# Four edits to a one-core decoder layer: part of product P2 next to P1 in the down projection, both parts of the compressed probabilities in one matmul, six row loads on ScalarE's queue, T sums written later

## The chip, the cores and the metric

The kernel runs on one core of a Trainium2 chip. The metric is device time in microseconds (us), the median of a few executions. The engines are named as in the profile: PE is TensorE's matmul, PEld its weight load, DVE is VectorE, ACT is ScalarE, POOL is GpSimd, SP is SyncE, whose queue issues most DMAs; "SPq" and "ACTq" are the queues of DMAs of SP and ACT.

## The reference

One decoder layer on x of 1024 rows by 1024 columns, all in float32: two attention mixers side by side, an output projection, a ConvFFN, and a gated per-layer embedding. Cut to what the change touches:

```
h = rmsnorm(x, g_pre_mix);  proj = h @ w_in
# NSA: 8 heads in 2 groups, three branches; the compressed one:
k_cmp, v_cmp = gelu(blocks(k) @ w1 + b1) @ w2, the same for v   # 63 blocks, head width 64
p_cmp = softmax(q k_cmp^T * scale - alibi) * mask;  o_cmp = p_cmp @ v_cmp
...                                              # selected and window branch, MLA, merge
x = x + rmsnorm(merged @ w_o, g_post_mix)
h = rmsnorm(x, g_pre_ffn)
u = causal_dwconv(h @ w_up, w_conv) + b_conv;  a, v = split(u)   # 2816 columns each
x = x + rmsnorm((gelu(a) * v) @ w_down, g_post_ffn)
e = p @ w_ple;  gate = sigmoid(x @ w_ple_gate)
x = x + rmsnorm(e * gate, g_ple)
```

## The kernel before

**Products in parts.** Every float32 operand of a large product is split into two rounded parts, hi and lo. ACT copies hi (`split_evac`, L308; for weights L106), DVE subtracts it for lo (L309; for weights L107), and `mm3` (L303 to L305) issues three matmuls: hi by hi, hi by lo, lo by hi. The three lines of `mm3` so stand for nearly all dense work of PE. DVE's row `wlo` or `wll` or `pl` is always the second half of such a split, and PE cannot use the part before it is there.

**Order.** The instructions of each engine come from a scheduler that orders the program by its own timeline; the source's order is an input to it, not the result. Tiles are taken from pools with a fixed number of buffers. PSUM tiles are `big` (two banks), `one`, `pT`, `oT`, `sc`.

**T sums.** The merge gates are computed by a seven-product (Strassen-like) scheme. Its sums T1 and T2 are made by `t_first(k)`, T3 and T4 by `t_second(k)`, for k from 0 to 3, on DVE and ACT, next to the projections of MLA's keys and values (`mla_k`, `mla_v`, some 120 to 190 us into the span). `st` is the tile into which MLA's projections are evacuated.

**Attention.** Units are one tile of 128 query rows by one group, with four heads (512 columns). `front` transposes the probabilities into PSUM (`pT`, L960) and splits them into `ph` and `pl`; `back` (L969, L970) multiplies both by the values and adds into `oT`. The unit's branch b = 0 is the compressed one: 64 rows of probabilities, and `Vc`, whose columns 0 to 63 hold the hi part of the values and columns 64 to 127 the lo part. There are 16 such units (8 row tiles by 2 groups).

**From w_o to the ConvFFN.** For eight tiles of 128 rows, in the order 4, 5, 6, 7, 0, 1, 2, 3: the row tile of x is loaded (`xt`, two buffers, L1402), `merged @ w_o` is accumulated, ACT squares it (L1359) for the norm, DVE multiplies by the norm and by `gpo` (L1410), adds `xt` (L1411), ACT squares `xt`, DVE multiplies by `gpf` (L1414), and PE transposes the result (L1370). `gpo` and `gpf` are rows of 1024 that are broadcast to 128 partitions by their loads (L1351, L1352, 512 KB each). Weights come through a ring of raw buffers, loaded on SP's queue (L81).

**Down projection.** A seven-product scheme on 2 by 2 blocks: P1, P5, P6, P3, P7, P4, P2, each of NJ = 11 units; a unit is a 128-deep slice, 12 matmuls of 128 by 512, into four banks. P1 is A11 B11 and P2 is A12 B21; their sum is the block c11 of the result. For each unit, `load` brings the blocks (through `wraw`, 3 buffers, or `QA`, `QS`, `GB`, which stay), `early_sums` makes the sums that P5, P6 and P7 need (L1544, on DVE; two for a P5 unit), and `ready` splits (ACT L308, DVE L309 `wlo`). After a product its four banks are added to or copied to `yacc`. Products P1, P6, P7, P2 take two `big` tiles, the others one `big` and two `one`. During P4 the weights of the gate (`wpg_items`) begin to come; after P4 the pool `qs` is closed, and the PLE inputs `praw`, `wlh`, `wll`, `pth`, `ptl` take its place; P2 runs beside their splits and transposes (`last_units`, `ple_in`, `fprep`). Then follow the PLE products and the gate's products.

Of the kernel before, what the change touches and what calls it, by code (L numbers as in the profile page):

```python
# [17 lines left out]
T = 1024  # L18
# [257 lines left out]
def tile_hybrid_layer(ctx: ExitStack, tc: tile.TileContext, x, p, positions, g_pre_mix, w_in,  # L276
# [679 lines left out]
    def front(u, key, cols, a, m=128):  # L956

        pT = bank().rearrange("p (a b) -> p a b", b=128)
        for r in range(a, 4):
            nc.tensor.transpose(pT[:m, r], cols(r), ident)  # L960
        tq = PL["tq"]
        ph = tq([128, 4, 128], F32R, "ph", bufs=3)
        pl = tq([128, 4, 128], F32R, "pl", bufs=3)
        split_evac(ph[:m, a:], pl[:m, a:], pT[:m, a:])
        u.hold[key] = (ph[:m, a:], pl[:m, a:])

    def back(u, key, oT, v, a, first, last):
        ph, pl = u.hold.pop(key)
        nc.tensor.matmul(oT[:, a:], v, ph, start=first, stop=False)  # L969
        nc.tensor.matmul(oT[:, a:], v, pl, start=False, stop=last)  # L970
# [6 lines left out]
    def nsa_unit(i, g, b):  # L977
# [107 lines left out]
        def t_back(j):  # L1085
            def run():
                if b == 1 and j == 0:
                    st["oT"] = new_oT()
                kb = k0 // 128 + j
                v = Vc[g][:64] if b == 0 else VV[kb // 4][:, kb % 4, 2 * (b - 1) + g]  # L1090
# [260 lines left out]
    nc.sync.dma_start(gpo, bcast_row(g_post_mix, D))  # L1351
    nc.sync.dma_start(gpf, bcast_row(g_pre_ffn, D))  # L1352
# [45 lines left out]
    for t in (4, 5, 6, 7, 0, 1, 2, 3):  # L1398
# [3 lines left out]
        nc.sync.dma_start(xt, x[0, ts, :])  # L1402
# [245 lines left out]

    def down_product(pi, per_unit):
        p_ = DOWN[pi]  # L1650
        if pi % 2:
# [4 lines left out]
        for j in range(NJ):  # L1656
            n = pi * NJ + j
# [4 lines left out]
            for m in range(2 * (n - 7), min(NJ, 2 * (n - 6))) if 7 <= n <= 12 else ():  # L1662
                early_sums(NJ + m)
            if n >= 13:
                early_sums(n + 9)
            ready(n + 4)
            per_unit(j)
            if n < 4 or n >= 15:
                load(n + 7)
            for m in range(2 * (n - 4), min(NJ, 2 * (n - 3))) if 4 <= n <= 9 else ():  # L1670
                load(NJ + m)
# [36 lines left out]
    for pi in range(1, 5):  # L1708
# [16 lines left out]
    down_product(5, lambda j: take(wpg_items[j // 2:j // 2 + 1]) if j % 2 and j < 10 else None)  # L1725
    qs.close()
# [16 lines left out]
    pp = Pool("pp", side="left")  # L1743
    praw = pp([128, NT, 256], F32, "praw")
    nc.sync.dma_start(praw, p[0, 0].rearrange("(t q) c -> q t c", q=128))
    wlh, wll = pp([128, 2, D], F32R, "wlh"), pp([128, 2, D], F32R, "wll")
    pth, ptl = pp([128, 2, T], F32R, "pth"), pp([128, 2, T], F32R, "ptl")
    for k, it in enumerate(ple_items):
        it.alloc = into(wlh[:, k], wll[:, k])
    ORDER = (4, 5, 6, 7, 0, 1, 2, 3)  # L1750
    for t in ORDER[:2]:
        x2_load(t)

    def ple_in(t):
        ps = one().rearrange("p (a b) -> p a b", b=128)
        for k in range(2):
            nc.tensor.transpose(ps[:, k], praw[:, t, k * 128:(k + 1) * 128], ident)
        ts = slice(t * 128, (t + 1) * 128)
        split_evac(pth[:, :, ts], ptl[:, :, ts], ps[:, :2])

    def last_units(j):
        if j in (1, 2):
            take(ple_items[j - 1:j])
        if j in (3, 5):
            fprep(ORDER[j // 2 - 1])
        if 6 <= j <= 9:
            ple_in(ORDER[2 * (j - 6)])
            ple_in(ORDER[2 * (j - 6) + 1])

    down_product(6, last_units)  # L1770
# [88 lines left out]
```

## Time and profile before

| | before |
|---|---|
| median of 3 runs | 1765.52 us (1764.72 to 1765.54) |
| profiled execution, its time | 1762.18 us |
| its span | 1760.5 us |
| its granted TensorE clock, mean | 0.994 |
| instructions | 23428 |
| busy PE, DVE, ACT, POOL | 1700.8, 1261.3, 853.0, 300.9 us |

Of the profiled execution's 1762.18 us, 1760.5 are the span of the trace; the 1.7 us around it are the same for any kernel here. The rows that the prediction reads from this trace stand below, numbered. In a timeline row "[1.40 <-DVE wlo L309]" means that the engine stood idle for 1.40 us before this instruction, and what ended the wait. PE's duration of one 128x512 matmul reads 0.39 us because matmuls are pipelined; in an unbroken run one starts every 0.23 us.

### The profile page before, as it was taken

To read this page: it belongs to the slowest core of one execution; us is meant where nothing else is said; L and a number is where in the kernel's file an instruction comes from. 1 tells how busy PE (TensorE), PEld (TensorE's weight loads), DVE (VectorE), ACT (ScalarE), POOL (GpSimd) and SP (SyncE) were. 2 spreads that over 40 slices of the span, in tenths; PEclk is the share of its full clock that TensorE was granted. 3 is DMA by queue.
4 is the path that set the end of the run, shared out by engine and by line. 5 is a ranking of instruction groups with operands and counts; after the bars stand their busy time and mean duration, and the time that the engine had idled before them with its cause. 6 is when DMAs were issued, how large, how long until landed. Compare 5 with 4: busy or idle time off the path is not lost.

```text
span 1760.5 us, 23428 instructions
## 1 busy us (share of the span) xinstructions
PE 1700.8 (97%) x8477; PEld 1390.7 (79%) x8477; DVE 1261.3 (72%) x1986; ACT 853.0 (48%) x1532; POOL 300.9 (17%) x435
## 2 busy tenths in 40 slices
PE   8999999999999999998999999999999998999998
PEld 6777888887777787886778877888888876887886
DVE  6577645238889777777754797888888789768553
ACT  6434433236777676666442454444444443335321
POOL 3000023014555553333211000000000000001111
PEclk9999999999999999999999999999999999999999
DMA  5176242100003236757362122232222292538111
GB/s 197 52 245 234 85 121 61 36 30 13 1 1 90 73 84 174 165 145 188 123 227 84 49 72 85 72 96 73 84 86 82 84 357 73 168 105 287 50 60 48
DMA packets 166670, 191.93 MB, mean 109 GB/s; under 512 B 13348, under 2 KB 116188, under 8 KB 166556
## 3 DMA queue, kind: packets, MB, share of 16 engines
q1 hardware_dynamic: 159452, 180.91, 33.1%
q10 hardware_dynamic: 7104, 9.54, 1.6%
q8 instruction: 67, 1.10, 0.3%
q14 instruction: 47, 0.39, 0.1%
HBM read 142.96 MB, written 47.45 MB: 108 GB/s over the span
## 4 chain that ended last, share of the span: by engine, by line
PE 80%; DVE 9%; DMA 6%; ACT 3%; issue 2%; POOL 1%; SPq 1%; DVEq 0%; POOLq 0%; ACTq 0%
PE big L304 9%; PE big L303 9%; PE big L305 9%; PE pT L303 6%; PE pT L305 6%; PE pT L304 6%; PE pT L960 5%; PE one L303 3%; PE one L304 3%; PE one L305 3%; PE oT L970 3%; PE oT L969 3%; DVE wlo L309 1%; PE sc L1023 1%; PE sc L1016 1%
## 5 line engine op out<-in xcount | busy, mean ns | idle before, releaser
L345 POOL TENSOR_SCALAR stat<-stat 128x1 f32<-128x1 f32 (+1 forms) x48 | 19.8, 412 | 892.1 <-ACT yn L1359 622.6
L308 ACT ACTIVATE ph<-pT 128x512 fp32r<-128x512 f32 (+1 forms) x244 | 130.2, 556 | 60.6 <-PE pT L960 52.5
L309 DVE TENSOR_TENSOR pl<-pT,ph 128x512 fp32r<-128x512 f32 (+1 forms) x244 | 149.6, 629 | 13.6 <-ACT ph L308 12.0
L303 PE MATMUL big<-hh,rh 128*128 128x512 f32 x380 | 148.2, 390 | 2.5 <-ACT e L220 1.0
L304 PE MATMUL big<-hl,rh 128*128 128x512 f32 x380 | 148.0, 389 | 0.0
L305 PE MATMUL big<-hh,rl 128*128 128x512 f32 x380 | 147.5, 389 | 0.0
L944 DVE TENSOR_REDUCE mx<-sc 128x1 f32<-128x640 f32 (+7 forms) x128 | 106.6, 835 | 32.1 <-PE sc L1023 22.3
L308 ACT ACTIVATE rh<-S 128x512 fp32r<-128x512 f32 x96 | 60.2, 629 | 110.3 <-PE big L304 78.0
L1482 DVE SCALAR_TENSOR_TENSOR u<-C,wcT,u 128x1024 f32<-128x1024 f32 x88 | 110.9, 1279 | 3.7 <-ACT u L1478 3.2
L304 PE MATMUL big<-wlo,whi 128*128 128x512 f32 x242 | 96.3, 398 | 9.3 <-DVE wlo L309 9.1
L303 PE MATMUL pT<-hh,whi 128*128 128x512 f32 x256 | 100.9, 394 | 3.0 <-DVE Vc L309 1.5
L308 ACT ACTIVATE rh<-wraw 128x512 fp32r<-128x512 f32 x80 | 50.0, 630 | 108.8 <-PE big L304 47.1
L305 PE MATMUL pT<-hh,wlo 128*128 128x512 f32 x256 | 100.7, 393 | 0.5 <-DVE wlo L107 0.5
L304 PE MATMUL pT<-hl,whi 128*128 128x512 f32 x256 | 100.3, 392 | 0.0
L305 PE MATMUL big<-whi,wlo 128*128 128x512 f32 x242 | 94.5, 390 | 0.0
L303 PE MATMUL big<-whi 128*128 128x512 f32 x242 | 90.8, 391 | 1.5 <-ACT whi L308 1.5
L303 PEld LDWEIGHTS big<-hh,rh 128*128 128x128 f32 x380 | 71.3, 188 | 18.6 <-ACT e L220 1.5
L304 PEld LDWEIGHTS big<-hl,rh 128*128 128x128 f32 x380 | 71.3, 188 | 15.1 <-DVE hl L309 0.4
L305 PEld LDWEIGHTS big<-hh,rl 128*128 128x128 f32 x380 | 71.3, 188 | 14.7
L309 DVE TENSOR_TENSOR rl<-S,rh 128x512 fp32r<-128x512 f32 x96 | 65.6, 686 | 19.5 <-ACT rh L308 19.5
L308 ACT ACTIVATE whi<-wraw 128x1024 fp32r<-128x1024 f32 x40 | 42.2, 1059 | 54.9 <-DVE wraw L1544 22.2
L304 PEld LDWEIGHTS big<-wlo,whi 128*128 128x128 f32 x242 | 45.4, 188 | 24.5 <-DVE wlo L309 15.5
(553 smaller groups left out, 4928.9 us busy)
## 6 DMA issues: line engine op xcount, KB each, us to landing
wraw<-in_w_up_dram SPq DMA_DIRECT2D x44, 512.0 KB, 3.9
wraw<-in_w_in_dram SPq DMA_DIRECT2D x24, 512.0 KB, 4.1
g<-gm_d SPq DMA_DIRECT2D x48, 256.0 KB, 4.1
wraw<-in_w_down_dram SPq DMA_DIRECT2D x47, 256.0 KB, 3.2
g_d<-u SPq DMA_DIRECT2D x22, 512.0 KB, 2.6
wraw<-g_d SPq DMA_DIRECT2D x36, 256.0 KB, 3.2
xt<-in_x_dram SPq DMA_DIRECT2D x16, 512.0 KB, 7.0
gm_d<-gms ACTq DMA_DIRECT2D x16, 512.0 KB, 2.6
```

What stands on the lines that cost most here:

```text
L303: nc.tensor.matmul(ps, lh, rh, start=start, stop=False, skip_group_check=more)
L304: nc.tensor.matmul(ps, lh, rl, start=False, stop=False, skip_group_check=more)
L305: nc.tensor.matmul(ps, ll, rh, start=False, stop=stop, skip_group_check=more)
L308: nc.scalar.activation(hi, ps, AF.Copy)
L309: nc.vector.tensor_sub(lo, ps, f32(hi))
L345: nc.gpsimd.tensor_scalar(st, st, EPS, None, op0=OP.add)
L944: nc.vector.tensor_reduce(u.nm[:, r:r + 1], src, axis=AX.XY, op=OP.max, negate=True)
L960: nc.tensor.transpose(pT[:m, r], cols(r), ident)
L969: nc.tensor.matmul(oT[:, a:], v, ph, start=first, stop=False)
L970: nc.tensor.matmul(oT[:, a:], v, pl, start=False, stop=last)
L1016: nc.tensor.matmul(ps[:, si, :w], qb[:, r], KB[b - 1][g][:, k0 + o:k0 + o + w], start=True, stop=False)
L1482: nc.vector.scalar_tensor_tensor(u[s], C[s][:, 2 - sh:2 - sh + T], wcT[:, 2 - sh, ch:ch + 1], u[s], op0=OP.mult, op1=OP.add)
```

## The change

Four edits, which do not touch each other:

- T sums: `t_first(0)` to `t_first(3)` are called later in the source.
- Compressed probabilities: DVE writes the lo part of the 64 rows into partitions 64 to 127 of `ph`, and `Vc` holds its columns twice, in rows 0 to 62 and 64 to 126; one matmul over 128 rows takes the place of two over 64.
- Row loads: `gpo`, `gpf` and the `xt` loads of tiles 4 and 5 are issued from ScalarE's queue.
- Down projection: P2's first 5 units stand right behind P1 and are added into P1's banks; its last 6 units stay at the end. P1 alone is copied to c21 first, P1 plus the 5 units to c11. The work that was spread beside 11 units of P2 is spread beside P4 and the last 6.

```diff
@@ T sums
     for i in range(4):
         for f in (mla_k(i, 0), mla_v(2 * i), mla_k(i, 1), mla_v(2 * i + 1)):
             f()
-        t_first(i)()
+        if i == 3:
+            t_first(0)()
         early.pop(0)()
+    t_first(1)()
...
     gates7 = Seven(nc, W, gate_pairs, ringA, BA, mm3, split_evac)
+    t_first(2)()
+    early.pop(0)()
+    t_first(3)()
+    early.pop(0)()
     for k in range(4):
         t_second(k)()
-        if k % 2:
-            early.pop(0)()
@@ compressed probabilities
-            split_evac(Vc[g][:63, 0:64], Vc[g][:63, 64:128], ps[:63, :64])
+            for o in (0, 64):
+                split_evac(Vc[g][o:o + 63, 0:64], Vc[g][o:o + 63, 64:128], ps[:63, :64])
...
+        if m == 64:
+
+            nc.scalar.activation(ph[:64], pT[:64], AF.Copy)
+            nc.vector.tensor_sub(ph[64:128], pT[:64], f32(ph[:64]))
+            u.hold[key] = [ph]
+            return
...
-        nc.tensor.matmul(oT[:, a:], v, ph, start=first, stop=False)
-        nc.tensor.matmul(oT[:, a:], v, pl, start=False, stop=last)
+        parts = u.hold.pop(key)
+        for j, part_ in enumerate(parts):
+            nc.tensor.matmul(oT[:, a:], v, part_, start=first and not j, stop=last and j == len(parts) - 1)
@@ row loads
-    nc.sync.dma_start(gpo, bcast_row(g_post_mix, D))
-    nc.sync.dma_start(gpf, bcast_row(g_pre_ffn, D))
+    nc.scalar.dma_start(gpo, bcast_row(g_post_mix, D))
+    nc.scalar.dma_start(gpf, bcast_row(g_pre_ffn, D))
...
-        nc.sync.dma_start(xt, x[0, ts, :])
+        (nc.scalar if 4 <= t < 6 else nc.sync).dma_start(xt, x[0, ts, :])
@@ down projection
-    DOWN = ("P1", "P5", "P6", "P3", "P7", "P4", "P2")
-    NJ = NF // 2
-    UNITS = [(p_, j) for p_ in DOWN for j in range(NJ)]
+    NJ, NP2 = NF // 2, 5
+    DOWN = [("P1", range(NJ)), ("P2", range(NP2))] + [(p_, range(NJ)) for p_ in ("P5", "P6", "P3", "P7", "P4")]
+    DOWN.append(("P2", range(NP2, NJ)))
+    UNITS = [(p_, j) for p_, js in DOWN for j in js]
...
+        p_, js = DOWN[pi]
+        more = pi == 1
+        if pi % 2 == 0 and pi:
             b = big()
             banks = [b[:, 0], b[:, 1], one(), one()]
-        else:
+        elif not more:
             banks = [b[:, h] for b in (big(), big()) for h in range(2)]
...
-                mm3(banks[t], hi[:, 0, lt], lo[:, 0, lt], hi[:, 1], lo[:, 1], j == 0, j == NJ - 1)
+                mm3(banks[t], hi[:, 0, lt], lo[:, 0, lt], hi[:, 1], lo[:, 1], i == 0 and not more,
+                    i == len(js) - 1, more)
...
             if p_ == "P1":
-                nc.scalar.activation(c11, ps, AF.Copy)
+                nc.scalar.activation(c21, ps, AF.Copy)
...
-                nc.vector.tensor_tensor(c21, c11, ps, op=OP.add)
+                nc.vector.tensor_tensor(c21, c21, ps, op=OP.add)
...
+            elif more:
+                nc.scalar.activation(c11, ps, AF.Copy)
...
-    down_product(6, last_units)
+    down_product(6, fourth)
+    down_product(7, last_units)
```

Three places show what the scheduler makes of it. On DVE, where MLA's projections are evacuated (`st`) and `t_first` makes T1 and T2 (L705 to L709), the changed kernel's order from its row 150 on:

```order
L705 TENSOR_TENSOR e<-hh_123,hh_125 128x512
L706 TENSOR_TENSOR e<-e,hl_124 128x512
L309 TENSOR_TENSOR st<-ta,st 128x512
L309 TENSOR_TENSOR st<-pT,st 128x512
L707 TENSOR_TENSOR e<-e,hl_126 128x512
L708 TENSOR_TENSOR t_1432<-hh_123,e 128x512
L309 TENSOR_TENSOR T1l<-e,T1h 128x512
```

The same rows stand in the same places in the kernel before; DVE's two orders first differ at row 371, which is a split of `Vc`.

On ACT, at the first w_o tiles (`hh<-g` is the last split of the merge, `big` the product of a row tile), of before and then of the change:

```order
L308 ACTIVATE hh_9196<-g_9382 128x512
L1359 ACTIVATE yt,stat<-big 128x1024 x2
L1359 ACTIVATE yt,stat<-xt 128x1024 x2
L308 ACTIVATE hh_8481<-one 128x4x128 x2
L1359 ACTIVATE yt,stat<-big 128x1024
```

```order
L308 ACTIVATE hh_9168<-g_9354 128x512
L1362 DMA gpo<-in_g_post_mix_dram 128x1024
L1363 DMA gpf<-in_g_pre_ffn_dram 128x1024
L1413 DMA xt<-in_x_dram 128x1024
L1370 ACTIVATE yt,stat<-big 128x1024
L1413 DMA xt<-in_x_dram 128x1024
L1370 ACTIVATE yt,stat<-big 128x1024
L1370 ACTIVATE yt,stat<-xt 128x1024 x2
```

The three loads now stand behind the last split of the merge and ahead of the first square; the second `xt` load stands between the squares of the two products.

On PE, where the down projection ends (`big<-wlo,whi` is P2, `wlh` and `pth` are the PLE product, `wgh` and `xh` the gate, `praw` the transposes of `ple_in`), of before and then of the change:

```order
L1757 MATMUL one<-ident,praw 128x128 x2
L305 MATMUL big<-whi,wlo 128x512
L303 MATMUL big<-whi 128x512
L304 MATMUL big<-wlo,whi 128x512
L305 MATMUL big<-whi,wlo 128x512
L303 MATMUL big<-whi 128x512
L304 MATMUL big<-wlo,whi 128x512
L305 MATMUL big<-whi,wlo 128x512
L303 MATMUL big<-whi 128x512
L304 MATMUL big<-wlo,whi 128x512
L305 MATMUL big<-whi,wlo 128x512
L303 MATMUL big<-wlh,pth 128x512
```

```order
L304 MATMUL big<-wlo,whi 128x512
L305 MATMUL big<-whi,wlo 128x512
L1785 MATMUL one<-ident,praw 128x128 x4
L303 MATMUL big<-wlh,pth 128x512
L304 MATMUL big<-wll,pth 128x512
L303 MATMUL big<-wgh_14647,xh 128x512
```

Before, the first transposes of `praw` stand inside P2, well ahead of the first PLE product; now they stand directly ahead of it, and only two PLE matmuls stand before the gate's.

## Rows read from the trace of the kernel before

**Rows 1.** The page, part 1: busy us, share and instructions of each engine.

```profile
PE 1700.8 (97%) x8477; PEld 1390.7 (79%) x8477; DVE 1261.3 (72%) x1986; ACT 853.0 (48%) x1532; POOL 300.9 (17%) x435
```

**Rows 2.** Stretches: length, busy us (instructions) by engine, clock, DMA share, GB/s.

```profile
400.00:680.00 280.00, 275.18 (x1767) 219.72 (x1765) 236.87 (x500) 202.76 (x477) 143.99 (x188) 1.00 0.20 55
880.00:920.00 40.00, 36.02 (x156) 29.46 (x155) 23.38 (x28) 17.15 (x27) 5.70 (x10) 0.96 0.74 239
1440.00:1480.00 40.00, 35.26 (x150) 27.29 (x149) 40.00 (x58) 17.70 (x21) 0.00 (x0) 1.00 0.45 159
1480.00:1520.00 40.00, 39.47 (x172) 31.54 (x171) 34.80 (x43) 14.49 (x14) 0.00 (x0) 1.00 0.31 103
```

**Rows 3.** Tile Vc, groups: count, duration in ns (least/median/most), first and last start.

```profile
L969 PE MATMUL oT<-ph,Vc x16: 491/497/502, 419.9 to 668.1; 64*128 64x512 f32 x16
...
L308 ACT ACTIVATE Vc<-pT x2: 208/213/218, 325.8 to 326.2; 63x64 fp32r<-63x64 f32 x2
```

**Rows 4.** PE's timeline: a K=128 product among dense matmuls (start, duration, instruction).

```profile
570.84 0.40 PE L969 MATMUL oT<-ph,V 128*128 128x512 f32 x1
571.08 0.39 PE L303 MATMUL pT<-hh,dh 128*128 128x512 f32 x1
```

**Rows 5.** PE's timeline: two products with Vc (K=64), one behind another, one alone.

```profile
443.98 0.39 PE L970 MATMUL oT<-pl,Vc 64*128 64x512 f32 x1
444.31 0.55 PE L960 MATMUL pT<-ident,hh 128*128 128x128 f32 x3
...
580.98 0.40 PE L305 MATMUL pT<-hh,dl 128*128 128x512 f32 x1
581.31 0.50 PE L969 MATMUL oT<-ph,Vc 64*128 64x512 f32 x1
581.74 0.50 PE L303 MATMUL pT<-hh,dh 128*128 128x512 f32 x1
```

**Rows 6.** DVE's timeline: the lo part for the products at 581.31 and 614.56.

```profile
579.31 0.68 DVE L309 TENSOR_TENSOR pl<-pT,ph 64x512 fp32r<-64x512 f32 x1
...
614.36 1.27 DVE L309 TENSOR_TENSOR pl<-pT,ph 64x512 fp32r<-64x512 f32 x2
```

**Rows 7.** PE's timeline: first and last of five waits in MLA's projections.

```profile
125.93 0.50 PE L303 MATMUL pT<-wvh,cth 128*128 128x512 f32 x1 [1.28 <-DVE st L309]
...
147.34 0.50 PE L303 MATMUL pT<-wvh,cth 128*128 128x512 f32 x1 [1.50 <-DVE st L309]
```

**Rows 8.** SP's queue: DMA issues, with the time each held the queue.

```profile
889.52 8.59 SPq L81 DMA_DIRECT2D wraw<-in_w_up_dram  x3
...
899.90 0.36 SPq L1351 DMA_DIRECT2D gpo<-in_g_post_mix_dram  x1
```

**Rows 9.** ACT's timeline: the last split of the merge.

```profile
895.95 0.63 ACT L308 ACTIVATE hh<-g 128x512 fp32r<-128x512 f32 x1 [1.53 <-DVE g L1287]
```

**Rows 10.** DVE's timeline at the first w_o tile.

```profile
905.15 1.28 DVE L1410 SCALAR_TENSOR_TENSOR yt<-big,stat,gpo 128x1024 f32<-128x1024 f32 x1 [6.83 <-DMA gpo<-in_g_post_mix_dram]
907.86 1.23 DVE L1411 TENSOR_TENSOR xt<-xt,yt 128x1024 f32<-128x1024 f32 x1 [1.43 <-DMA xt<-in_x_dram]
```

**Rows 11.** PE's timeline at the first w_o tile.

```profile
913.65 1.97 PE L1370 MATMUL one<-ident,yt 128*128 128x128 f32 x8 [3.56 <-DVE yt L1414]
```

**Rows 12.** PE: first and last of five waits, P5 and P6; one in P2.

```profile
1454.59 0.50 PE L304 MATMUL big<-wlo,whi 128*128 128x512 f32 x1 [1.40 <-DVE wlo L309]
...
1490.57 0.50 PE L304 MATMUL big<-wlo,whi 128*128 128x512 f32 x1 [0.53 <-DVE wlo L309]
...
1607.85 0.50 PE L304 MATMUL big<-wlo,whi 128*128 128x512 f32 x1 [1.37 <-DVE wlo L309]
```

**Rows 13.** DVE's timeline: the last lo part of a gate weight.

```profile
1638.81 1.22 DVE L309 TENSOR_TENSOR wlo<-wraw,whi 128x1024 fp32r<-128x1024 f32 x1
```

**Rows 14.** PE's timeline: first PLE product, first use of the last gate weights.

```profile
1635.30 0.39 PE L303 MATMUL big<-wlh,pth 128*128 128x512 f32 x1
...
1645.75 0.40 PE L303 MATMUL big<-whi,xh 128*128 128x512 f32 x1
```

More of the change, by code (lines that the diff above doesn't have):

```diff
@@ L962, in front @@
         ph = tq([128, 4, 128], F32R, "ph", bufs=3)
+        if m == 64:
[3 more added lines that the diff above has]
+            return
         pl = tq([128, 4, 128], F32R, "pl", bufs=3)
-        split_evac(ph[:m, a:], pl[:m, a:], pT[:m, a:])
-        u.hold[key] = (ph[:m, a:], pl[:m, a:])
+        split_evac(ph[:, a:], pl[:, a:], pT[:, a:])
+        u.hold[key] = [ph[:, a:], pl[:, a:]]
     def back(u, key, oT, v, a, first, last):
-        ph, pl = u.hold.pop(key)
-        nc.tensor.matmul(oT[:, a:], v, ph, start=first, stop=False)
-        nc.tensor.matmul(oT[:, a:], v, pl, start=False, stop=last)
+        parts = u.hold.pop(key)
+        for j, part_ in enumerate(parts):
+            nc.tensor.matmul(oT[:, a:], v, part_, start=first and not j, stop=last and j == len(parts) - 1)
     st = {}
@@ L1089, in run @@
                 kb = k0 // 128 + j
-                v = Vc[g][:64] if b == 0 else VV[kb // 4][:, kb % 4, 2 * (b - 1) + g]
+                v = Vc[g] if b == 0 else VV[kb // 4][:, kb % 4, 2 * (b - 1) + g]
                 back(u, j, st["oT"], v, 0, b == 1 and j == 0, b == 0)
@@ L1493, in conv_pieces @@
                 [lambda: tap(1, 1)], [lambda: tap(1, 2)], [out_], []]
-    DOWN = ("P1", "P5", "P6", "P3", "P7", "P4", "P2")
-    NJ = NF // 2
-    UNITS = [(p_, j) for p_ in DOWN for j in range(NJ)]
+    NJ, NP2 = NF // 2, 5
+    DOWN = [("P1", range(NJ)), ("P2", range(NP2))] + [(p_, range(NJ)) for p_ in ("P5", "P6", "P3", "P7", "P4")]
+    DOWN.append(("P2", range(NP2, NJ)))
+    UNITS = [(p_, j) for p_, js in DOWN for j in js]
+    AT = {u: n for n, u in enumerate(UNITS)}
+    N5, N6 = AT["P5", 0], AT["P6", 0]
     QA, QS, GB, LOADED = {}, {}, {}, {}
@@ L1647, in part @@
         return yacc[:, t, cols]
+    banks = None
     def down_product(pi, per_unit):
-        p_ = DOWN[pi]
-        if pi % 2:
+        nonlocal banks
+        p_, js = DOWN[pi]
+        more = pi == 1
+        if pi % 2 == 0 and pi:
             b = big()
             banks = [b[:, 0], b[:, 1], one(), one()]
-        else:
+        elif not more:
             banks = [b[:, h] for b in (big(), big()) for h in range(2)]
-        for j in range(NJ):
-            n = pi * NJ + j
+        for i, j in enumerate(js):
+            n = AT[p_, j]
             hi, lo = unit.pop(n)
@@ L1660, in down_product @@
                 lt = slice(t * 128, (t + 1) * 128)
-                mm3(banks[t], hi[:, 0, lt], lo[:, 0, lt], hi[:, 1], lo[:, 1], j == 0, j == NJ - 1)
-            for m in range(2 * (n - 7), min(NJ, 2 * (n - 6))) if 7 <= n <= 12 else ():
-                early_sums(NJ + m)
-            if n >= 13:
+                mm3(banks[t], hi[:, 0, lt], lo[:, 0, lt], hi[:, 1], lo[:, 1], i == 0 and not more,
+                    i == len(js) - 1, more)
+            if 0 <= n - 7 < NJ:
+                early_sums(N5 + n - 7)
+            if n + 9 >= N6:
                 early_sums(n + 9)
             ready(n + 4)
-            per_unit(j)
-            if n < 4 or n >= 15:
+            per_unit(i)
+            if n + 7 < N5 or n + 7 >= N6:
                 load(n + 7)
-            for m in range(2 * (n - 4), min(NJ, 2 * (n - 3))) if 4 <= n <= 9 else ():
-                load(NJ + m)
+            if 0 <= n - 4 < NJ:
+                load(N5 + n - 4)
         for t, ps in enumerate(banks):
@@ L1707, in tile_hybrid_layer @@
     down_product(0, last_conv)
-    for pi in range(1, 5):
+    for pi in range(1, 6):
         down_product(pi, nothing)
@@ L1724, in tile_hybrid_layer @@
     W.stop = W.pos + len(early_items)
-    down_product(5, lambda j: take(wpg_items[j // 2:j // 2 + 1]) if j % 2 and j < 10 else None)
-    qs.close()
     X2, X3, X3T = {}, {}, {}
@@ L1741, in fprep, with fourth @@
         X3T[t] = (xh, xl)
[L1743 to L1749, printed above, removed]
-    ORDER = (4, 5, 6, 7, 0, 1, 2, 3)
-    for t in ORDER[:2]:
-        x2_load(t)
+    ORDER = (4, 5, 6, 7, 0, 1, 2, 3)
+    PP = {}
+    def fourth(i):
+        if i % 2 and i < 10:
+            take(wpg_items[i // 2:i // 2 + 1])
+        if i == 7:
+            qs.close()
+            pp = PP["pool"] = Pool("pp", side="left")
+            PP["praw"] = praw = pp([128, NT, 256], F32, "praw")
+            nc.sync.dma_start(praw, p[0, 0].rearrange("(t q) c -> q t c", q=128))
+            PP["wl"] = wlh, wll = pp([128, 2, D], F32R, "wlh"), pp([128, 2, D], F32R, "wll")
+            PP["pt"] = pp([128, 2, T], F32R, "pth"), pp([128, 2, T], F32R, "ptl")
+            for k, it in enumerate(ple_items):
+                it.alloc = into(wlh[:, k], wll[:, k])
+            for t in ORDER[:2]:
+                x2_load(t)
     def ple_in(t):
@@ L1756, in ple_in, with last_units @@
         for k in range(2):
-            nc.tensor.transpose(ps[:, k], praw[:, t, k * 128:(k + 1) * 128], ident)
+            nc.tensor.transpose(ps[:, k], PP["praw"][:, t, k * 128:(k + 1) * 128], ident)
         ts = slice(t * 128, (t + 1) * 128)
[L1759 to L1768, printed above, removed]
-    down_product(6, last_units)
+        split_evac(*(a[:, :, ts] for a in PP["pt"]), ps[:, :2])
+    def last_units(i):
+        if i < 2:
+            take(ple_items[i:i + 1])
+        if i in (1, 3):
+            fprep(ORDER[i // 2])
+        if i > 1:
+            ple_in(ORDER[2 * (i - 2)])
+            ple_in(ORDER[2 * (i - 2) + 1])
+    down_product(6, fourth)
+    down_product(7, last_units)
+    pp, (wlh, wll), (pth, ptl) = PP["pool"], PP["wl"], PP["pt"]
     W.stop = len(W.items)
```

## The prediction

> **What bounds the kernel now.** I read first the page's busy times: PE is busy 97% of the span, DVE 72%, ACT 48% [rows 1]. A kernel like this gets faster in two ways: PE has less to do, or one of its few waits goes. So I listed next PE's busy time in stretches of 40 us and then, in PE's timeline, the idle time before each instruction. Four places bear on the change. In the attention (400 to 680 us) PE is busy 275.18 of 280 us and DVE 236.87 [rows 2], so work taken from PE there shortens the span nearly one for one. At the first w_o tile PE stands for 3.56 us [rows 11], in a stretch whose granted clock is 0.96 against 1.00 elsewhere [rows 2]. In P5 and P6 PE waits five times for the lo part of a split, 5.3 us in all [rows 12], while DVE is busy 40.00 of 40 us [rows 2]: there DVE is the bound. In MLA's projections PE waits five times for the evacuation `st`, 4.9 us in all [rows 7].
>
> What a wait costs beyond its idle time: the row of a matmul lasts 0.39 us where the next starts 0.23 us on [rows 4], so "idle" begins 0.16 us late, and the first row behind a wait reads 0.50 [rows 12] instead of 0.39. I charge each wait its idle time plus 0.27.
>
> **T sums.** The order of DVE's instructions is the same before and after from the first row to row 371, and that place lies behind all T sums. The later calls in the source do not come through to the engine. The five waits stay: 0. If they did go, they would be worth 4.9 + 5 x 0.27 = 6.2 us.
>
> **Compressed probabilities.** 16 pairs of matmuls, hi and lo (the hi ones in [rows 3], the lo ones have the same form), become 16 single ones. The least that this saves is an unbroken start to start interval each: 16 x 0.23 = 3.7 us. But these 64-row products cost more than that. One behind another they start 0.33 us apart, and one alone among dense matmuls takes 0.43 us to the next start and comes 0.10 us late itself [rows 5], 0.53 in all, while a 128-row product in the same surroundings takes 0.24 [rows 4]. The new product has 128 rows, and I take it at 0.23. Seven of the 16 pairs stand together in the timeline and nine apart; a pair together saves 2 x 0.33 - 0.23 = 0.43, one apart 2 x 0.53 - 0.23 = 0.83, in all 3.0 + 7.5 = 10.5 us, the upper bound. Against it: the single product needs both parts, where now the first needs only what ACT writes. For the product at 581.31 DVE's part was done at 579.99, 1.3 us ahead; at 614.56 it was not, its two rows run from 614.36 to 615.63 [rows 6]. Three units stand like that, some 0.5 us each. So I take 7 us, the middle of the two bounds. ACT and DVE move no more elements per unit than before.
> The second copy of `Vc` adds two ACT and two DVE instructions of 0.21 us [rows 3] at 326 us, where PE waits for `Vc` already: at most the 0.4 us of one engine's pair, since the two engines work side by side: 0.4 taken.
>
> **Row loads.** Now SP's queue stands for 8.59 us in three weight loads, the last of which waits for a ring buffer, and the load of `gpo` comes only at 899.90 [rows 8]. It lands at 905.15, DVE having waited 6.83 us; the `xt` load lands at 907.86 after 1.43 more [rows 10], and PE's transposes follow 5.8 us behind that, at 913.65 [rows 11]. PE's last matmul before them so began at 909.70 (3.56 us of wait and 0.39 of its own before 913.65). The changed order has the loads on ACT's queue behind the last split of the merge, which ended at 896.58 [rows 9]: 3.3 us earlier for `gpo`, and `gpf` and `xt` right behind it. The bytes are the same, and the weight loads that were held until 898 come in between. 3.3 us earlier `gpo` lands at 901.9; `xt`, no longer last, I put at 903.5 to 904.5. The 5.8 us behind it lead to 909.3 to 910.3 for the transposes: the wait is gone or below 0.3 us.
> A price: the second `xt` load stands on ACT ahead of two squares and waits for its turn among the loads, to about 903; ACT's squares are then needed from 904.7 on, so it costs nothing unless that load waits 1.7 us longer than I put it.
> What the wait is worth: 3.56 idle plus 0.27, plus what the clock took behind it (eight transposes in 1.97 us [rows 11], about 1 us above what eight at full clock would take, half of their time). That is 4.8 us; the lower bound is 0. I take 4.5.
> The Trainium skill speaks against this edit: "DMA: Bandwidth & Descriptors", section "Issuing engines are not separate DMA queues", says that loads started from several engines run on the same 16 DMA engines and that a second queue saves only the issuing time. By that the edit would be worth the issue of four loads, 1.4 us, and the sum below 12.5. The row of 8.59 us is not issue but a wait that holds the queue, so I hold the measurement higher; no run here has shown the loads on the other queue yet.
>
> **P2 next to P1.** The number of matmuls is unchanged. Five units of 12 matmuls put 5 x 12 x 0.23 = 13.8 us of PE work ahead of P5, and bring five more splits to DVE, each a 128x1024 instruction of 1.22 us as in [rows 13], 6.1 us. The P5 sums are so due 7.7 us later against the work that precedes them, and the five waits come to 5.3 us in all. They should go: 5.3 + 5 x 0.27 = 6.6 us. DVE is then still nearly full there (by the windows, 75 us busy of 80 between 1440 and 1520 [rows 2]; five more splits against 13.8 us more room), so I take 5.5; the lower bound is 0.
> Adding the five units into P1's banks puts a new wait on PE: ACT must have read a bank first. The changed order gives PE three units into the first two banks before it touches the other two, 18 matmuls or 4.1 us, against 0.6 us per copy: 0. Four more copies on ACT, at 17.70 busy of 40 [rows 2]: 0.
> The wait of 1.37 us in P2 [rows 12] comes from the step out of P4, which keeps its order: it stays.
> At the end P2's last part covers 6 x 12 x 0.23 = 16.6 us, and some 3 more with the transposes and waits, where 11 units covered 30. Behind it come the gate's products, whose last weight was split at 1640.03 [rows 13], 4.7 us after P2's end (the first PLE product started at 1635.30) and 5.7 us before the first use of that group of weights at 1645.75 [rows 14]. If these splits kept their distance to P4, they would come 13.8 us late against P2's end and PE would wait 13.8 - 5.7 = 8.1 us. But five units' splits fewer stand ahead of them on DVE and ACT, and the ring comes free sooner; what I see for certain is that two PLE matmuls stand directly behind the transposes that they need, ACT's copy of 0.4 to 0.6 us between. I take a loss of 1 us; bounds 0 and 8.1. What moves from P2 into the gate's stretch is hidden by DVE's idle time there (at 1638.81 DVE splits the last gate weight, with only a few splits of `pth` behind it).
>
> **Sum**, against the profiled execution: 7 - 0.4 + 4.5 + 5.5 - 1 = 15.6 us, from 1762.18 to 1746.6. The median of the runs is 3.3 us above the profiled time, so by the same difference 1749.9. I predict **1750 us**, 0.9% less. Half of the sum is work that leaves PE for good (the products), the other half waits that may come back elsewhere.
>
> **Rivals.**
> - *The end of the down projection becomes the bound.* The loss of 1 us is 8.1, the sum 8.5, the time 1757. For: P2 covers half as much. Against: DVE and ACT have less ahead of those splits. 0.13.
> - *The loads land no sooner from ACT's queue.* The DMA engines are busy 0.74 of that stretch [rows 2], and what is gained for `gpo` is lost to the weight loads beside it. The sum falls by 4.5 to 11, the time is 1754. Against: the engines' idle time when SP's queue stands. 0.13.
> - *DVE stays full and the waits only move behind P2's part.* Sum 10, time 1755. Against: 7.7 us of slack for 5.3 of waits. 0.08.
> - *The T sums do move.* 6.2 us more: 1744. Against: the unchanged order. 0.02.
> - *Slower:* each of the 16 products waits for its DVE part, since it cannot start on ACT's part alone. A wait of w costs 16 x (w + 0.27); it outweighs the sum and 3.5 us more from w = 0.92 us on. At w = 1.2 it costs 23.5 us, and the time is 1773. For: the pair of rows at 614.36 [rows 6]. Against: 13 of 16 have DVE's part ahead by up to 1.3 us. 0.05.
>
> **How the numbers follow.** 0.55 for the forecast, which alone spans 1744 to 1756 by the bounds of the products (3.7 to 10.5) and of the DVE waits; the remaining 0.04 is for two losses together. A measurement of this kernel can tell a change of about 0.2%, 3.5 us. Faster needs more than that, which all cases but the slower one and the combined losses give: 0.86; same 0.08; slower 0.06. The range reaches from 1743 (upper bounds) to 1760 (the two dearest losses together, 4.5 + 7.1 of the sum, which leaves 4.0, and 1.5 for the low end of the products' price).
>
> **What would show it.** In the trace after: 16 products with `Vc` of 128 rows, with starts 0.23 to 0.3 apart from their neighbours; `gpo` landed near 902 and no wait above 1 us before the first transposes of w_o; PE's idle time between 1440 and 1500 below 1.5 us; the five waits for `st` unchanged; at the first gate product a wait below 2 us. I would be wrong if the products wait for `ph` each time, if ACT stands behind its own loads so that the squares come late, or if the gate's first weights come after P2's end by more than their slack.

## The result and the profile after

The changed kernel took 1753.24 us (median of 4 runs, 1752.29 to 1754.87) against 1765.53 us before in the same runs: a ratio of 0.9935, 95% interval 0.9922 to 0.9948, so 11.5 us faster (9 to 14). Predicted were 1750 us and 15.6 us of gain. When the change ran once more among the experiments it gave 1751.94 us, ratio 0.9932 (0.9915 to 0.9949). The edit moves four loads (`gpo`, `gpf`, and `xt` of tiles 4 and 5), not the six that the title counts. What lies outside the span of a trace is 1.9 us in the four runs of the changed kernel and 1.7 in that of before, so it is not quite the same for every kernel.

The page of the changed kernel, part 1 [rows 1], and the four stretches of [rows 2]; the attention now starts about when it did and ends some us earlier, so the same window holds more of the work behind it:

```profile
PE 1696.0 (97%) x8461; PEld 1393.6 (79%) x8461; DVE 1263.1 (72%) x1988; ACT 855.5 (49%) x1538; POOL 299.5 (17%) x435
```

```profile
400.00:680.00 280.00, 271.82 (x1792) 222.99 (x1791) 245.18 (x511) 206.99 (x487) 146.36 (x190) 1.00 0.21 60
880.00:920.00 40.00, 37.74 (x169) 30.56 (x168) 22.05 (x26) 14.41 (x26) 4.88 (x12) 0.96 0.68 221
1440.00:1480.00 40.00, 40.00 (x178) 33.13 (x177) 39.27 (x54) 19.60 (x23) 0.00 (x0) 1.00 0.48 170
1480.00:1520.00 40.00, 38.36 (x169) 31.43 (x168) 37.27 (x48) 15.23 (x15) 0.00 (x0) 1.00 0.32 106
```

PE is now busy all of the 40 us in P5's stretch, where it lost 4.74 of them before; the one wait that is left falls in the next stretch. At the first w_o tile it still loses 2.26, and the clock of that stretch is 0.96 as before.

**Where the time went.** The start of the same instruction in both traces tells how far the changed kernel is ahead. At the first attention product it is 0.50 us late (402.01 against 401.51), at the end of attention 6.49 ahead (846.16 against 852.65), at the first up projection 8.13 ahead (966.68 against 974.81), at the place in P1 from which the down projection runs alone 8.08 (1405.90 against 1413.98; the first two units of P1 run earlier, inside the up projection), at the end of the span 7.5 (1753.0 against 1760.5). So the attention won 7.0 us, the w_o stretch 1.6, and the down projection and all behind it lost 0.6. Ahead of the attention 1.58 us are won up to 140 us, where both kernels have the same instructions, and 2.07 are lost from 326 us on. The two profiled executions lie 7.5 us apart in span, the medians of the runs 12.3; what this difference is, the fourth experiment shows.

PE over the whole attention, in the trace of before and in that of the change:

```profile
401.50:852.80 451.30, 438.62 (x2697) 352.68 (x2696) 370.02 (x761) 314.39 (x729) 206.06 (x260) 1.00 0.36 94
```

```profile
402.00:846.30 444.30, 429.41 (x2681) 351.18 (x2680) 372.08 (x761) 314.20 (x729) 207.88 (x260) 0.99 0.37 95
```

PE's work there fell by 9.2 us, and its idle time grew from 12.7 to 14.9, so 7.0 are left.

The group of tile `Vc` [rows 3] and PE's timeline at two of its products [rows 5], behind transposes and behind score products (`sc`):

```profile
L981 PE MATMUL oT<-ph,Vc x16: 392/477/501, 420.4 to 663.1; 128*128 128x512 f32 x16
L308 ACT ACTIVATE Vc<-pT x4: 208/216/218, 324.3 to 326.2; 63x64 fp32r<-63x64 f32 x4
```

```profile
444.25 0.48 PE L981 MATMUL oT<-ph,Vc 128*128 128x512 f32 x1
444.57 0.60 PE L965 MATMUL pT<-ident,hh 128*128 128x128 f32 x4
...
580.73 0.39 PE L981 MATMUL oT<-ph,Vc 128*128 128x512 f32 x1
580.96 1.25 PE L965 MATMUL pT<-ident,pS 128*128 128x128 f32 x10
```

16 products over 128 rows. The second of these takes 0.23 us to the next start, as six of the 16 do; nine, like the first one here, take 0.32 to 0.34, eight of them behind transposes; one has a wait behind it.

PE's timeline behind the copies of `Vc`, changed kernel:

```profile
326.56 0.47 PE L303 MATMUL pT<-hh,whi 128*128 128x512 f32 x1 [1.99 <-DVE KBc L840]
...
327.86 0.63 PE L305 MATMUL pT<-hh,wlo 128*128 128x512 f32 x1
328.28 0.63 PE L303 MATMUL pT<-hh,whi 128*128 128x512 f32 x1
328.71 0.63 PE L304 MATMUL pT<-hl,whi 128*128 128x512 f32 x1
```

The wait is 1.99 us where it was 1.50, and behind it eight matmuls, the last at 330.84, start 0.43 us apart instead of 0.23: the granted clock is 0.50 there, PE at 1.2 instead of 2.4 GHz. That is 0.5 us of wait and 1.6 of clock.

The row loads, on ACT's timeline, DVE's first addition of `xt` [rows 10], and PE's first transposes of w_o [rows 11]:

```profile
888.62 0.34 ACTq L1362 DMA_DIRECT2D gpo<-in_g_post_mix_dram  x1
...
890.00 0.44 ACTq L1413 DMA_DIRECT2D xt<-in_x_dram  x1
...
899.26 0.34 ACTq L1413 DMA_DIRECT2D xt<-in_x_dram  x1
899.65 1.03 ACT L1370 ACTIVATE yt<-big 128x1024 f32<-128x1024 f32 x1 [7.53 <-DMA wraw<-in_w_up_dram]
...
900.66 1.05 ACT L1370 ACTIVATE yt<-xt 128x1024 f32<-128x1024 f32 x1
```

```profile
897.92 1.23 DVE L1422 TENSOR_TENSOR xt<-xt,yt 128x1024 f32<-128x1024 f32 x1 [3.49 <-DMA xt<-in_x_dram]
```

```profile
904.32 1.78 PE L1381 MATMUL one<-ident,yt 128*128 128x128 f32 x8 [2.00 <-DVE yt L1425]
```

`gpo` is there in time: DVE's first product with it starts at 893.15 and waits only for the norm from POOL. But ACT stands 7.53 us behind the second `xt` load, which by the trace waits until a weight load has landed. DVE had finished tile 4's `xt` at 899.15; its square ran only at 900.66, behind the square of the second product, which ACT had also held back.

DVE's and ACT's part at the end of the down projection shows on PE's timeline (changed kernel; the first row answers to the five waits of [rows 12]):

```profile
1486.38 0.50 PE L304 MATMUL big<-wlo,whi 128*128 128x512 f32 x1 [1.64 <-DVE wlo L309]
...
1610.02 0.50 PE L304 MATMUL big<-wlo,whi 128*128 128x512 f32 x1 [1.74 <-DVE wlo L309]
...
1623.59 0.50 PE L303 MATMUL big<-wlh,pth 128*128 128x512 f32 x1 [1.36 <-ACT pth L308]
...
1625.02 0.80 PE L303 MATMUL big<-wgh,xh 128*128 128x512 f32 x1 [0.70 <-DVE yacc L1712]
1625.62 0.63 PE L304 MATMUL big<-wgl,xh 128*128 128x512 f32 x1
```

Of five waits one is left; the row at 1610.02 is the wait of P2 that was there before. Where P2's last part ends there are two new ones, and half clock again behind them.

The idle times do not show all of what P5 and P6 won. From the first matmul of P5 to the first of P3, 264 matmuls in either kernel, before and after:

```profile
1441.47:1509.30 67.83, 62.56 (x265) 48.78 (x264) 63.50 (x86) 27.16 (x29) 0.00 (x0) 1.00 0.36 124
```

```profile
1448.72:1510.51 61.79, 60.15 (x265) 49.47 (x264) 59.06 (x78) 27.16 (x30) 0.00 (x0) 1.00 0.32 107
```

That is 6.0 us less, where the waits alone went from 5.3 to 1.6: before, five more units began late by up to 0.1 us and had a slow first matmul (0.34 us to the next start), and as a row lasts 0.39 us where the next starts 0.23 us on, this reads as no idle time.

### The profile page after: what moved, and what is told of

Same layout as the page of the kernel before. It is cut to its first block, busy times and chain, and to the rows that moved or that the text cites. A ratio compares the mean times of both kernels' runs of the same rounds, so it can differ in the third digit from the quotient of the medians.

```text
span 1753.0 us, 23383 instructions
## 1 busy us (share of the span) xinstructions
PE 1696.0 (97%) x8461; PEld 1393.6 (79%) x8461; DVE 1263.1 (72%) x1988; ACT 855.5 (49%) x1538; POOL 299.5 (17%) x435
## 4 chain that ended last, share of the span: by engine, by line
PE 80%; DVE 9%; DMA 4%; ACT 3%; issue 3%; POOL 0%; SPq 0%; DVEq 0%; ACTq 0%; POOLq 0%
PE big L303 10%; PE big L304 10%; PE big L305 10%; PE pT L303 6%; PE pT L305 6%; PE pT L304 6%; PE oT L981 5%; PE pT L965 4%; PE one L303 3%; PE one L304 3%; PE one L305 3%; DVE wlo L309 1%; PE sc L1034 1%; PE sc L1027 1%; DVE QS L1559 1%
## 5 line engine op out<-in xcount | busy, mean ns | idle before, releaser
L309 DVE TENSOR_TENSOR pl<-pT,ph 128x512 fp32r<-128x512 f32 x228 | 139.1, 626 | 11.5 <-ACT ph L308 9.6
L308 ACT ACTIVATE ph<-pT 128x512 fp32r<-128x512 f32 x228 | 120.8, 554 | 47.6 <-PE pT L965 36.0
L309 DVE TENSOR_TENSOR rl<-wraw,rh 128x512 fp32r<-128x512 f32 x80 | 54.6, 686 | 11.4 <-ACT rh L308 11.4
```

The costliest lines, as they stand in the source:

```text
L308: nc.scalar.activation(hi, ps, AF.Copy)
L309: nc.vector.tensor_sub(lo, ps, f32(hi))
```

## The experiments

Each kernel ran in turns with the kernel before; ratios are to it, with the 95% interval. It reaches 0.001 to 0.002 to either side, 2 to 3.5 us.

**1. Compressed probabilities alone.** The diff is that part of the change.

```diff
+            for o in (0, 64):
+                split_evac(Vc[g][o:o + 63, 0:64], Vc[g][o:o + 63, 64:128], ps[:63, :64])
...
+            nc.scalar.activation(ph[:64], pT[:64], AF.Copy)
+            nc.vector.tensor_sub(ph[64:128], pT[:64], f32(ph[:64]))
...
```

> Only the compressed probabilities of the change (one product of 128 rows, Vc written twice). Theory 1, from the two traces: the attention gains 7.0 us and the two more copies of Vc lose 2.1 (0.5 of wait and 1.6 of half clock behind it), so 5 us faster, about 1760.5. Rival, the prediction's own sizes: 7 less 0.4, so 6.6 us faster, about 1759. In the trace a wait of about 2 us on DVE KBc at 326 us, and whether the granted clock falls behind it.

Measured: 1756.63 us against 1763.63, ratio 0.9965 (0.9952 to 0.9979), 6 us faster (4 to 8.5). In its trace the attention wins 7.1 us (from 0.4 late to 6.7 ahead at 663 us) and 2.1 are lost at 326 us, as in the change. Both theories are inside the interval. In this execution the lead grows further behind 663 us, to 8.3 at the end of attention; how far these totals agree between traces stands in the table of the next section.

**2. P2's part alone.**

```diff
+    NJ, NP2 = NF // 2, 5
+    DOWN = [("P1", range(NJ)), ("P2", range(NP2))] + [(p_, range(NJ)) for p_ in ("P5", "P6", "P3", "P7", "P4")]
+    DOWN.append(("P2", range(NP2, NJ)))
...
```

> Only P2's first five units next to P1. Theory 1, from the two traces: what the waits in P5 and P6 give (about 5 us) is given back where P2's short last part ends (two waits of 1.4 and 0.7 us and 1.5 us of half clock) and by the transposes that moved behind it: 0 to 1 us faster, about 1765. Rival, the prediction: 5.5 less 1, so 4.5 us faster, about 1761.

Measured: 1761.58 us against 1763.63, ratio 0.9988 (0.9977 to 1.0), 2 us (0 to 4). The first theory is inside the interval, the predicted 4.5 outside. In the trace one wait of 1.73 us is left in P5 and P6, which together take 62.1 us against 67.8 before: 5.8 won there, and most of it lost again behind them.

**3. Row loads alone.**

```diff
-    nc.sync.dma_start(gpo, bcast_row(g_post_mix, D))
+    nc.scalar.dma_start(gpo, bcast_row(g_post_mix, D))
...
-        nc.sync.dma_start(xt, x[0, ts, :])
+        (nc.scalar if 4 <= t < 6 else nc.sync).dma_start(xt, x[0, ts, :])
```

> Only the row loads on ScalarE's queue. Theory 1, from the two traces: the wait before the first transposes is 2 us instead of 3.6, so 1.6 to 2.8 us faster, about 1763.3. Rival, the prediction: the wait is gone, 4.5 us faster, 1761. Second rival: no sooner landing, 1765.5.

Measured: 1762.51 us against 1763.63, ratio 0.9994 (0.9985 to 1.0002), 1 us. The predicted 4.5 is out. The wait before the transposes is 3.14 us, and ACT's timeline shows 7.64 us of standing behind the second `xt` load. From the first w_o product to the first up projection this trace takes as long as that of before (116.61 us against 116.64).

**4. T sums alone.** A kernel whose engines have the same instructions in the same order as before.

```diff
-        t_first(i)()
+        if i == 3:
+            t_first(0)()
...
```

> Only the T sums written later. Theory 1 and the prediction: every engine's order is that of the kernel before, so the same time within 0.1%, 1765.5; its trace is a second execution of that program, and what differs between the two traces is what executions of one program differ by. Rival: 6 us faster, 1759, with no waits for st between 125 and 148 us.

Measured: 1764.69 us against 1763.63, ratio 1.0007 (0.9996 to 1.0017): no change. PE's timeline of this run still has all five waits [rows 7]; the first and the last, and then the place at 326 us:

```profile
123.47 0.50 PE L303 MATMUL pT<-wvh,cth 128*128 128x512 f32 x1 [1.27 <-DVE st L309]
...
145.98 0.50 PE L303 MATMUL pT<-wvh,cth 128*128 128x512 f32 x1 [1.02 <-DVE st L309]
```

```profile
326.26 0.79 PE L303 MATMUL pT<-hh,whi 128*128 128x512 f32 x1 [1.50 <-DVE Vc L309]
326.85 0.63 PE L304 MATMUL pT<-hl,whi 128*128 128x512 f32 x1
327.28 0.63 PE L305 MATMUL pT<-hh,wlo 128*128 128x512 f32 x1
```

This is the second trace of the program of before, and it differs from the first: 2.45 us earlier near 75 us, 1.1 later by 155 us, 1.4 later behind the wait at 326 us (same wait, this time with half clock behind it), 2.4 later at the step from P4 to P2. One execution so says what each wait is, but not to 2 or 3 us what a program takes.

Most of what executions differ by goes with the granted clock, which is known for every run, traced or not. Over the 32 runs of the kernel before, beside these first four experiments, the mean granted clock lies between 0.988 and 0.995, and the time falls with it by 1.4 us per 0.001 (correlation -0.86). The traced run of before had 0.994, that of the change 0.990, the longest of its four. By this slope the two are an estimated 5.6 us apart in clock alone, about the 4.8 us between the difference of the two spans and that of the medians. So the medians are the fair measure of the change, and the two traces understate it.

**5. The change once more.** No edit.

> The change itself once more, beside the three kernels below and for a second trace of it. If what two traces of one program differ by is the start, the half clock behind waits and transfers (as the runs of the T sums alone showed, whose instructions are those of before), this one again comes out 10 to 13 us faster than before, 1751 to 1754, and the attention's 7 us and the two waits at the end of P2's last part stand in its trace again, while the half clock behind the wait at 326 us may or may not.

Measured: 1751.94 us against 1763.88, ratio 0.9932 (0.9915 to 0.9949). The attention wins 5.6 us from its first product (2.1 late) to 663 us (3.5 ahead) and 1.4 more up to its end, 7.0 in all; there are waits of 1.99 at 326 us and 2.20 before the transposes; at the end of P2 one wait of 0.32 and one of under 0.3 us, not 1.36 and 0.70. So the size of the end's waits is one of the things that vary.

**6. The second row load back on SP's queue.**

```diff
-        (nc.scalar if 4 <= t < 6 else nc.sync).dma_start(xt, x[0, ts, :])
+        (nc.scalar if t == 4 else nc.sync).dma_start(xt, x[0, ts, :])
```

> The change, but the second xt load (tile 5) on SP's queue again. Theory 1: ACT stands 7.5 us behind that load, so the square of tile 4 comes about 2.6 us after its data, behind the square of the second product; without it the wait of 2 to 3 us before the first transposes falls below 1 us, and with it the half clock behind it goes: 2 to 4 us faster than the change, about 1750. Rival: it is the first xt load itself that lands late because it shares the transfer with gpo, gpf and the weights; then the wait stays at 2 us or more and the time at the change's.

Measured: 1749.31 us against 1763.88, ratio 0.9917 (0.9901 to 0.9933), 2.6 us better than the change in the same runs, with overlapping intervals. The trace decides: ACT's square of tile 4 starts as DVE's addition ends, PE's transposes follow the matmul ahead of them, without a wait and at full clock, and the stretch 880 to 920 has clock 1.00.

```profile
900.37 1.23 DVE L1422 TENSOR_TENSOR xt<-xt,yt 128x1024 f32<-128x1024 f32 x1 [2.60 <-DMA xt<-in_x_dram]
```

```profile
901.63 1.06 ACT L1370 ACTIVATE yt<-xt 128x1024 f32<-128x1024 f32 x1 [4.38 <-DVE xt L1422]
```

```profile
904.78 0.39 PE L304 MATMUL big<-wlo,hh 128*128 128x512 f32 x1
905.12 1.09 PE L1381 MATMUL one<-ident,yt 128*128 128x128 f32 x8
```

```profile
880.00:920.00 40.00, 38.94 (x179) 31.42 (x180) 23.48 (x28) 15.57 (x28) 4.86 (x12) 1.00 0.76 229
```

The rival (the first load itself is late) falls: the same holds in all five traces with this edit, and the square comes 1.4 to 2.6 us late in all five with the load on ACT's queue. The clock of the stretch does not decide it: the trace of experiment 5 had a wait of 2.20 us and full clock behind it.

**7. The second copy of Vc out of SBUF.**

```diff
-            for o in (0, 64):
-                split_evac(Vc[g][o:o + 63, 0:64], Vc[g][o:o + 63, 64:128], ps[:63, :64])
+            split_evac(Vc[g][:63, 0:64], Vc[g][:63, 64:128], ps[:63, :64])
+            nc.scalar.activation(Vc[g][64:127], Vc[g][:63], AF.Copy)
```

> The change, but the second copy of Vc is read from the first one (two ACT instructions in SBUF) and not from PSUM. Theory 1: the longer wait at 326 us (1.99 against 1.50) comes from the further reads of the PSUM tile that stand ahead of PE's next use, so it falls back to 1.5 us and 0.5 us are won; the half clock behind it comes or not as before. Rival: the wait is for KBc alone and stays at 2.0.

Measured: 1752.99 us against 1763.88, ratio 0.9936 (0.9921 to 0.9951), no difference that can be measured. In the trace the wait is back at 1.50 us, and in this execution no half clock followed. The cause of the 0.5 us is shown, its worth is below what the runs can tell. Over all traces half clock followed each of the five waits of 1.98 to 1.99 us at this place, and three of the nine of 1.50.

**8. Three units instead of five.**

```diff
-    NJ, NP2 = NF // 2, 5
+    NJ, NP2 = NF // 2, 3
...
-        if i > 1:
+        if 1 < i < 6:
...
```

> The change with 3 units of P2 next to P1 and 8 at the end. Theory 1: the loss at the end comes from too short a last part (the transposes of the PLE input and P2's four additions stand directly ahead of the PLE and gate products); with 8 units the two waits (2.1 us) and the half clock behind them (1.5) go, while 3 x (2.76 - 1.22) = 4.6 us of slack still nearly cover the 5.3 us of waits in P5 and P6: 2 to 4 us faster than the change, about 1750. Rival: DVE is full at the end whatever the split, and the waits stay; then the same as the change, or slower by the P5 waits that come back (up to 2 us).

Measured: 1754.01 us against 1763.88, ratio 0.9937 (0.9919 to 0.9955), the same as the change within the intervals. The two waits before the PLE and gate products are gone, and one wait of 1.13 us is left in P5 and P6, but at the step from P4 to P2's last part PE waits 3.58 us for ACT:

```profile
1601.80 1.22 PE L303 MATMUL big<-whi 128*128 128x512 f32 x2 [3.58 <-ACT whi L308]
```

ACT stood there 5.55 us behind the split of a gate weight (`wgh<-gt`), whose load had been issued 10 us before. In the other traces this wait is between none (the change) and 1.71 us, in that of before 0.53.

**9. The compressed probabilities and the row loads with the two mends, without the P2 part.** The T sums are left as before, which no engine sees.

```diff
+        (nc.scalar if t == 4 else nc.sync).dma_start(xt, x[0, ts, :])
...
+            nc.scalar.activation(Vc[g][64:127], Vc[g][:63], AF.Copy)
```

> Compressed probabilities (second copy of Vc from SBUF) and row loads with tile 5's load on SP's queue, without the move of P2's part: what stands here against the next kernel is the worth of that part alone. Theory 1, from six traces: it wins 4.5 us in P5 and P6 and gives back most of it at the end, 0.7 us on the mean (-0.6 to 1.5): this kernel 0 to 2 us slower than the next. Rival, the prediction's size: 4.5 us slower than the next.

Measured: 1752.22 us against 1766.39, ratio 0.9928 (0.9911 to 0.9945).

**10. The change with the two mends** (the edits of experiments 6 and 7 together).

> The change with tile 5's load on SP's queue and the second copy of Vc from SBUF. By the runs of each alone: the wait before the first transposes of w_o gone, 0.5 us less at 326 us: 1749 to 1750, 14 us faster than before.

Measured: 1749.41 us against 1766.39, ratio 0.9909 (0.9889 to 0.9929). Against the ninth the P2 part is worth 2.8 us by medians, with intervals that overlap; that agrees with the 2 us of the second run.

**11. The same with four units** (`NP2 = 4`).

> The kernel just above with 4 units of P2 next to P1 and 7 at the end. Theory 1: the slack ahead of P5 is 4 x (2.76 - 1.22) = 6.2 us against 6.3 of waits, and the last part is 2.8 us longer: the waits of 0.7 and 0.5 us before the PLE and gate products go, so 1 to 2 us faster than with 5. Rival: what is won there is lost at the step out of P4, where the run with 3 units had a wait of 3.6 us: the same time within 1 us.

Measured: 1748.53 us against 1766.39, ratio 0.9906 (0.9886 to 0.9925): the same time within what the runs tell. Its trace has one wait of 1.13 us in P5 and P6 and none before the PLE and gate products, as the theory had it, but the time does not show that it is faster.

**12. Three additions from DVE to POOL.**

```diff
-        nc.vector.tensor_add(x3, x3, X2.pop(t))
+        (nc.gpsimd if t in ORDER[:3] else nc.vector).tensor_add(x3, x3, X2.pop(t))
```

> All with mends, and three additions of 128x1024 (x plus the normed output, first three tiles) taken from DVE to POOL at the end of the down projection. Theory 1: DVE, full from 1610 to 1628 us, is what P2's last part waits for (the wait of 1.74 us on wlo and the 0.3 to 0.7 us before PLE and gate): with 2.4 us less on DVE there 1 to 2 us faster than without. Rival: the waits come from transfers and ACT's order (the gate weight that ACT waits for at the step out of P4): the same time, or slower if POOL's additions take longer than DVE's and PE's transposes wait for them.

Measured: 1754.83 us against 1766.39, ratio 0.994 (0.9923 to 0.9958), 5 us worse than the tenth by medians. POOL takes 2.38 to 3.22 us for an addition that DVE does in 1.22, and the small steps of the norms that stand behind it on POOL come later; the wait before the first PLE product is longer, not shorter:

```profile
1625.40 0.50 PE L303 MATMUL big<-wlh,pth 128*128 128x512 f32 x1 [2.70 <-ACT pth L308]
```

So this does not show whether DVE's full load is what the end waits for. That stays open.

## Why the prediction held, and where its steps were off

The time came out inside the range, near the forecast, and the gain at 11.5 to 12 us instead of 15.6. The range is wide, and its upper end of 1760 us is counted from the profiled execution; counted from the median, as the forecast is, the same sum gives 1763. The time lies inside either way.

The same stretches, measured in all traces, in us (in brackets how many traces):

| stretch | without that edit | with it |
|---|---|---|
| attention, first product to last | 448.3 to 451.3 (4) | 442.4 to 444.7 (10) |
| first w_o product to first up projection | 116.1 to 116.8 (4) | 113.5 to 116.6 (5); with the second `xt` load on SP's queue 110.4 to 114.1 (5) |
| P5 and P6 | 67.80 to 67.85 (5) | 61.8 to 62.5 (9) |
| from P3 to the end, plus the units moved to P1 | 251.1 to 253.6 (5) | five units: 254.3 to 256.2 (6, without experiment 12) |

Step by step:

- **T sums: 0.** Right. The kernel with this edit alone has before's order and took the same time, and four waits for `st`, 3.5 to 4.1 us in all, stand in every trace. The fifth of the five in the prediction, 0.79 us at 135.01, is not for `st` but for ACT's `gms`.
- **Compressed probabilities: 7.** Right in size: 6.4 us on the mean of the traces, 6 us net by the runs. But 7 was the middle of two bounds. In the pair of traces the work that left PE is 9.2 us, near the upper bound (10.5; six pairs stand together and ten apart, not seven and nine, which makes it 10.9), and 2.2 came back as longer waits in the attention: score products waited 3.1 us for ACT's `hl` instead of 1.0, a term that the sum did not have. That the middle was met is in part luck. The saving is where it was put: behind transposes a 64-row product starts 0.20 us after the last of them and takes 0.43 to the next start, a 128-row one mostly 0.03 and 0.32; elsewhere it takes 0.23 where the 64-row ones took 0.33 to 0.53. The slower rival (each product waits for DVE) did not come. The second copy of `Vc` cost 0.5 us of wait for 0.4 predicted, and in all five traces with that wait 1.3 to 1.6 us of half clock behind it, which I had not priced.
- **Row loads: 4.5.** The step that failed is the price of the second `xt` load, which "costs nothing unless that load waits 1.7 us longer than I put it". I had put its issue at about 903 on the clock of the trace of before. It came at 899.26 in the changed kernel, which was 6.6 us ahead there, so at about 906: 3 us longer, and the square of tile 4 ran 1.5 us behind its data (2.6 in experiment 3). The first `xt` load came at the late end of what I had put (903.5 to 904.5): DVE's addition at 897.92 is 904.6 on that clock. A second thing is missing from the step: in the changed order PE comes to the transposes five matmuls, 1.1 us, earlier, so the same lateness is a longer wait. Gained were 1 us by the runs (experiment 3) and 1.7 on the mean of the traces. With that one load on SP's queue the wait is gone, and the stretch is 4.6 us shorter than before on the mean, as predicted for the whole edit. The page of the Trainium skill that I had weighed ("DMA: Bandwidth & Descriptors", section "Issuing engines are not separate DMA queues") gives the second queue only the issuing time. The prediction put that at 1.4 us, and for the edit as it stands the runs cannot tell 1 us from it; the 4.6 us without the second `xt` load are more, since `gpo` no longer stands behind a wait on SP: DVE's wait of 6.83 us for it [rows 10] is gone.
- **P2 next to P1: 5.5 - 1.** The 5.5 are right: P5 and P6 take 5.9 us less on the mean of the traces, though DVE is still busy 59.06 of 61.79 us there. The term that was mis-sized is the loss at the end, put at 1: from P3 on the kernels with five units take 3.3 us more on the mean. Part of it are the two waits behind P2's last part, 0.6 (experiment 5) to 2.1 us (the change), and half clock behind them (granted clock 0.96 from 1600 to 1640 us, 1.00 before); what the rest is stays open. What is left is 2 to 3 us by the runs (experiments 2, 9 and 10) and 2.6 by the traces. The accumulation into P1's banks cost nothing, as predicted.

The larger misses go one way, to less gain. Of the signs named ahead, the waits for `st` and that of the first gate product (0.70 us) came about as described, and the products nearly (nine stand 0.32 to 0.34 apart from the next, not up to 0.3); the wait before the w_o transposes (2.00 us instead of below 1) did not, and PE's idle time in P5 and P6 (1.64 instead of below 1.5) just missed.

The sum of the parts measured alone is 6 + 2 + 1 + 0 = 9 us with some 2 us of uncertainty each, the whole 11.5 to 12. They agree within that. The best kernel here (four units, both mends) is 0.9906 of before; it is not shown to be faster than the one with five.

## What to carry to other kernels

A load that is moved to the queue of an engine which also computes holds up all that stands behind it on that engine for as long as the load has to wait for its turn: move only loads that can be issued at once. When work is moved ahead of a place where an engine is full, look at what that work had been covering; here the splits and transposes at the end lost half of their cover, and more than half of what the move had won. Time a stretch from the first start of one product to the first start of another, and not by its idle times alone: short delays of a pipelined engine read as no idle time. And from an edit of the source read first whether it reaches the engines at all: the T sums did not.

## What the runs showed of the hardware

- Executions of one and the same program spread wider than the runs of before first showed: 32 of the kernel before lay between 1758.54 and 1768.26 us. Traces of one program differ by 1 to 3 us at a few places: at transfers, and behind waits. Most of the spread goes with the mean granted clock, 1.4 us per 0.001.
- After one and the same wait of 1.50 us PE ran on at 2.4 GHz in the trace of before, and at 1.2 GHz for about six matmuls in that of experiment 4. What decides between them these runs don't show; the price was 1.3 to 1.6 us each time.
- A matmul over 64 rows among matmuls over 128 took 0.53 us of PE's time, one behind another 0.33, one over 128 rows 0.23 (up to 0.34 behind transposes).
- POOL took 2.38 to 3.22 us for an addition of 128x1024 in float32, DVE 1.22.
